# Output tiles counted until stored, z projections and the residual gate across periods, new durations in an own scheduler

## The chip, the cores and the metric

The kernel runs on one core of one Trainium2 chip. The metric is the device time of one execution in microseconds, lower is better. Three runs of the kernel before took 1211.33, 1213.61 and 1215.69 us; the median is 1213.61.

## The reference

One layer (DEPTH is 1, so the gated DeltaNet alone) on x of 1024 x 1024, all float32:

```python
mod = silu(c) @ ada_w + ada_b;  shift, scale, gate = split(mod, 3)
h = rms_norm(x, norm_g) * (1 + scale) + shift
qkv, z, b_lin, a_lin = split(h @ w_in)            # 8 q/k heads, 16 v heads of 128
qkv = silu(causal_conv(qkv, conv_w))              # 4 taps
q, k = l2norm(q) * 128**-0.5, l2norm(k)           # each used by 2 value heads
beta = sigmoid(b_lin);  g = -exp(a_log) * softplus(a_lin + dt_bias)
gc = cumsum(g) in a chunk; decay = exp(gc_i - gc_j)
t_mat = inverse(I + strictly_lower(beta k k^T * decay))
for chunk:                                        # state S, 128 x 128 for a head
    v_new = u - w @ S;  o = q_dec @ S + qk @ v_new
    S = S * exp(g_last) + k_dec^T @ v_new
out = rms_norm(x + gate * ((rms_norm(o, norm_w) * silu(z)) @ w_out), final_g)
```

## The kernel before

The heads are worked in eight **pairs** (two value heads that share one q/k head), numbered 0 to 7. Chunks of 128 tokens give each pair eight scan steps. Products in float32 precision of the big matrices are three passes of 128x512 matmuls on split values (`whi`, `wlo` and the high and low halves of h): a tile of 128 columns and 512 tokens is 24 matmuls (L598, "projection matmuls").

**Stages of a pair.** Its k and q tiles (4 projections) and v tiles (4) pass a convolution on VectorE (three steps L557 a tile, after L552 and L554 on ScalarE, before the SiLU L561), and are transposed (k and q L659, L667; v L813, then `vtok` L816). `stage_a` takes products of k and q (L704) and makes eight `at` tiles in two halves (L706, L710). They go to DRAM (D<-at, L715) and come back in another layout (`ua`, L724). On `ua` VectorE inverts 32 x 32 blocks in 62 dependent steps (L733 and L736 in turn, of growing and shrinking size). The result goes through DRAM (D<-tb L738, TT<-D L755), is transposed (L758 to L760), and `levels` joins the blocks to 128 x 128 on TensorE (L766, L768, L778, L779, L789, L797 with copies between), for one half of the tokens and then for the other. Then the pair's `scan` may start: a step is L963, L982, L940, L973, L910 on TensorE with small VectorE and ScalarE work between.

**The scan's output.** After a step the output `o` is normed; `finish` transposes it into the PSUM bank `pot` (L892), ScalarE writes `oT` (L896), GpSimd multiplies it by `z` (L897), and SyncE stores it to `o_dram` (L898). `pot` has one buffer, `oT` two, and up to ZB = 3 tiles of z are fetched ahead. `out_gate` makes z for a head: two projections, SiLU (L868), a store to `z_dram` (L865).

**The residual gate** is gate = silu(c) @ ada_w's third part: for each of eight column tiles two loads of 256 KB (`wag`, L1007), eight products on VectorE (L1011, L1013), a sum (L1016), a reduction on TensorE (L1020) and an add (L1022); at the end a transpose (L1026). `wag` has one buffer (WGB), and a tile's first load waits for the tile before.

**The order.** All five engines take their instructions in the order in which the program emits them. A planner sets it in Python. Work is written as generators that yield None after a matmul or a condition to wait for. `drive` steps the first generator of a list that can go on; a clock `now` advances by a matmul's cost. VectorE, ScalarE, GpSimd and SyncE operations go into queues (`put`) with a cost, a rank and the operations they come after; `advance` emits from each queue, at the planned time, the ready operation of lowest rank. `done` asks if an operation ended LATP ago, `avail` if a tag has a buffer whose readers are done. The costs are AC, VC, LAT, DMA and the numbers beside the calls.

**Periods.** The outer loop has nine periods gi = -1 to 7. In a period the scan of pair gi, `stage_a` of pair gi + 1 and, as filler, projections run: the z heads of the period (ZQ gives 3, 2, 2, 2, 2, 2, 2, 1, 0 of them), the v tiles of pair gi + 1 and the k and q tiles of pair gi + 2. A period ends when all its generators in `must` are over. `residual_gate` is in `must` of period RG = 1. In period 6 `early` (output products L1066 of the first four heads) may take NE = 15 steps behind the fillers; it runs free in period 7. After the periods the rest of the output product follows: 768 matmuls in all, L1066.

## Time and profile before

| | |
|---|---|
| profiled execution, its own time | 1215.66 us |
| its span, first to last instruction | 1213.9 us |
| TensorE matmul busy | 1090.0 us (90%) |
| VectorE / ScalarE / GpSimd busy | 752.1 / 542.3 / 436.0 us |
| mean granted TensorE clock | 0.947 |
| SyncE's queue q1 | 117.15 MB, 33.8% of 16 engines' span |

The time is the slowest core's, here the only one's, and the span is the part of it between the first and the last instruction. The engines overlap, so their busy times do not add up. A matmul's row covers its passage through the array: matmuls start every 0.23 us while each row lasts 0.4, and "busy" is the time that at least one covers. The granted clock is 1.0 at 2.4 GHz and 0.5 at 1.2 GHz; a mean in between is a mix of both.

### The profile page before, as it was taken

How to read it: one execution, taken by the hardware profiler on the slowest of the kernel's cores; microseconds unless marked ns; L12 is line 12 of the kernel's file. 1: busy time of each engine (PE TensorE's matmuls, PEld its weight loads, DVE VectorE, ACT ScalarE, POOL GpSimd, SP SyncE). 2: the span in 40 equal slices, each digit the busy share in tenths (PEclk: the TensorE clock that was granted, in tenths of full speed). 3: DMA queues.
4: the chain of work that ended last, by engine and by line, in shares of the span. 5: the costliest groups of instructions: out<-in, count | busy, mean ns of one | idle time of the engine just before them, and what ended most of it. 6: DMA issues, size and time to landing. Idle time of an engine off the chain costs nothing.

```text
span 1213.9 us, 18304 instructions
## 1 busy us (share of the span) xinstructions
PE 1090.0 (90%) x6295; PEld 870.9 (72%) x6295; DVE 752.1 (62%) x1913; ACT 542.3 (45%) x1415; POOL 436.0 (36%) x530
## 2 busy tenths in 40 slices
PE   8998986999998949999899989998998849999997
PEld 7877764777776737777677767776776637788775
DVE  5457864685758747766586767586665854512614
ACT  5466821443652326336623733473365312514433
POOL 3442320431452215313521442163126123754653
PEclk8899996999998969999999989998999878999999
DMA  9712141241243421421424042214213260536441
GB/s 291 194 35 96 32 119 31 70 117 45 79 125 90 107 72 55 127 61 58 109 61 118 19 125 61 84 45 125 62 57 107 88 198 17 182 102 183 152 130 70
DMA packets 187555, 118.43 MB, mean 98 GB/s; under 512 B 59669, under 2 KB 166470, under 8 KB 186438
## 3 DMA queue, kind: packets, MB, share of 16 engines
q1 hardware_dynamic: 186960, 117.15, 33.8%
q8 instruction: 50, 0.82, 0.3%
q14 instruction: 43, 0.35, 0.1%
q10 hardware_dynamic: 502, 0.10, 0.0%
HBM read 91.98 MB, written 25.24 MB: 97 GB/s over the span
## 4 chain that ended last, share of the span: by engine, by line
PE 46%; DVE 18%; ACT 15%; DMA 8%; issue 6%; POOL 5%; SPq 2%; DVEq 0%; POOLq 0%; ACTq 0%
PE pj L598 24%; PE pj L1066 3%; DVE tm L733 2%; DVE vT L557 2%; DVE tb L736 2%; DMA woraw<-in_gdn_w_out 2%; DVE kq L557 2%; DVE em L641 2%; PE tr L797 2%; POOL wolo L206 2%; PE tr L789 2%; ACT tr L669 2%; DMA o_dram<-oT 2%; ACT tr L662 1%; ACT junk L918 1%
## 5 line engine op out<-in xcount | busy, mean ns | idle before, releaser
L587 POOL TENSOR_TENSOR wlo<-wraw,whi 128x512 fp32r<-128x512 f32 x88 | 116.2, 1336 | 317.1 <-ACT whi L586 305.0
L733 DVE TENSOR_TENSOR tm<-tb,ua 128x126 f32<-128x126 f32 (+22 forms) x248 | 88.7, 358 | 52.7 <-DMA ua<-D 46.4
L557 DVE SCALAR_TENSOR_TENSOR kq<-xb,taps,kq 128x512 f32<-128x512 f32 x96 | 78.3, 825 | 30.4 <-ACT kq L554 23.5
L557 DVE SCALAR_TENSOR_TENSOR vT<-xb,taps,vT 128x512 f32<-128x512 f32 x96 | 78.3, 816 | 20.0 <-ACT vT L554 19.0
L736 DVE TENSOR_TENSOR tb<-tb,tm 128x126 f32<-128x126 f32 (+22 forms) x248 | 83.8, 338 | 7.1
L552 ACT COPY xb<-pj 128x512 f32<-128x512 f32 x62 | 36.3, 585 | 101.1 <-PE pj L598 97.4
L598 PE MATMUL pj<-h0hib,wlo 128*128 128x512 f32 x184 | 79.0, 429 | 0.0
L598 PE MATMUL pj<-h0hib,whi 128*128 128x512 f32 x184 | 78.4, 426 | 0.0
L598 PE MATMUL pj<-h0hia,whi 128*128 128x512 f32 x184 | 77.0, 418 | 1.3 <-ACT kq L554 1.3
L598 PE MATMUL pj<-h0lob,whi 128*128 128x512 f32 x184 | 77.8, 423 | 0.0
L598 PE MATMUL pj<-h1hib,wlo 128*128 128x512 f32 x184 | 77.3, 420 | 0.0
L598 PE MATMUL pj<-h1loa,whi 128*128 128x512 f32 x184 | 77.1, 419 | 0.0
L598 PE MATMUL pj<-h1hib,whi 128*128 128x512 f32 x184 | 76.4, 415 | 0.0
L598 PE MATMUL pj<-h1hia,wlo 128*128 128x512 f32 x184 | 76.0, 413 | 0.0
L922 POOL TENSOR_TENSOR sso<-sso,neg_half 128x2 f32<-128x2 f32 x64 | 45.0, 705 | 84.9 <-DVE sso L920 76.1
L598 PE MATMUL pj<-h1lob,whi 128*128 128x512 f32 x184 | 75.4, 410 | 0.0
L598 PE MATMUL pj<-h0loa,whi 128*128 128x512 f32 x184 | 75.1, 408 | 0.0
L598 PE MATMUL pj<-h1hia,whi 128*128 128x512 f32 x184 | 74.8, 407 | 0.0
L598 PE MATMUL pj<-h0hia,wlo 128*128 128x512 f32 x184 | 74.6, 406 | 0.0
L951 POOL TENSOR_TENSOR sg<-st,eall 128x256 f32<-128x256 f32 x48 | 30.2, 629 | 103.8 <-ACT st L985 103.8
L206 POOL TENSOR_TENSOR wolo<-woraw,wohi 128x512 fp32r<-128x512 f32 x36 | 48.1, 1356 | 46.8 <-ACT wohi L205 46.8
L897 POOL TENSOR_TENSOR oT<-oT,z 128x256 f32<-128x256 f32 x64 | 47.7, 746 | 45.1 <-ACT oT L896 44.1
(460 smaller groups left out, 2930.9 us busy)
## 6 DMA issues: line engine op xcount, KB each, us to landing
wraw<-in_gdn_w_in SPq DMA_DIRECT2D x92, 256.0 KB, 3.6
woraw<-in_gdn_w_out SPq DMA_DIRECT2D x50, 256.0 KB, 3.0
wa<-in_ada_w SPq DMA_DIRECT2D x16, 512.0 KB, 7.1
em<-gc_dram SPq DMA_DIRECT2D x8, 1024.0 KB, 5.3
z_dram<-sz SPq DMA_DIRECT2D x32, 256.0 KB, 2.4
z<-z_dram SPq DMA_DIRECT2D x64, 128.0 KB, 2.4
o_dram<-oT SPq DMA_DIRECT2D x64, 128.0 KB, 2.2
gsrc<-o_dram SPq DMA_DIRECT2D x32, 256.0 KB, 3.1
```

Source lines behind the costliest of these rows:

```text
L206: nc.gpsimd.tensor_tensor(lo, raw, hi.bitcast(F32), op=ALU.subtract)
L552: a = act(lambda: nc.scalar.copy(xb[:, NTAP - 1:], ps), 512, *old, rank=0, holds=held)
L557: d = [vec(lambda j=j: nc.vector.scalar_tensor_tensor(dst, xb[:, j:j + TH], tp[:, j], dst, op0=ALU.mult, op1=ALU.add), 512, *d)]
L587: ops.append(pool(lambda raw=raw, ks=ks, hi=hi, lo=lo: nc.gpsimd.tensor_tensor(lo[:, ks], raw, hi[:, ks].bitcast(F32), op=ALU.subtract), 1 ...
L598: nc.tensor.matmul(ps, lhsT=a[:, k], rhs=b[half][k // 4][:, k % 4], start=(k == 0 and n == 0), stop=(k == KT - 1 and n == 2))
L641: e = [vec(lambda n=n, h=h: nc.vector.scalar_tensor_tensor(em[:, h, n], em[:, h, n], ngc[:, n, h0 + h:h0 + h + 1], mask, op0=ALU.add, op1= ...
L733: d = [vec(lambda j=j, mm=mm, ln=ln, tmv=tmv: nc.vector.tensor_tensor(tmv, tb[:, :mm, j:j + 1].to_broadcast([P, mm, ln]), ua[:, j:j + 1, j ...
L736: d = [vec(lambda j=j, mm=mm, tmv=tmv: nc.vector.tensor_tensor(tb[:, :mm, j + 1:], tb[:, :mm, j + 1:], tmv, op=ALU.subtract), 170 + mm * l ...
L897: b = pool(lambda: nc.gpsimd.tensor_tensor(oT, oT, z, op=ALU.mult), 800, a, zo)
L922: d = pool(lambda: nc.gpsimd.tensor_tensor(sso, sso, neg_half[:, :2], op=ALU.pow), 700, d)
L951: sgo = pool(lambda n=n, sg=sg: nc.gpsimd.tensor_tensor(sg, st, gle[:, n, hs, None].to_broadcast([P, 2, P]), op=ALU.mult), 800, rank=0)
L1066: nc.tensor.matmul(acc, lhsT=a[:, ts], rhs=b, start=(first and n == 0), stop=(last and n == 2))
```

## The change

- `oT` gets three buffers (OB), and a buffer counts as taken until its store is over (`order.hold("oT", 1)`, asked in `can_finish`); in the kernel before the planner did not ask. z tiles fetched ahead: ZB 5 for 3.
- The z heads of each period become a run of their own (`zruns`). Their own period still needs them (`follow` steps the run to its end), and the period before may work on them when nothing else can go on.
- `residual_gate` runs in the background, in no period's `must`. `wag` has two buffers (WGB = 2), and a load waits for the operations of the load two before; a first product waits for the tile before.
- `early` runs without a quota from period 6 on (`take` and the NE steps are gone).
- Planned durations: LAT is 200 (150) between engines and 50 on one engine, LATP 320 (250), some costs of ScalarE and VectorE, and the 62 inversion steps 220 + n/2 (170 + 3n/4).
- The builder's `dynamic_dma_scratch_size` is set to 1024.

```diff
-LAG, ZB, WGB = 3, 3, 1
+LAG, ZB, WGB, OB = 3, 5, 2, 3
-LAT, LATP, DMA = 150, 250, 2800
+LATS, LAT, LATP, DMA = 50, 200, 320, 2800
-AC = {512: 530, 256: 400, 128: 240}
-VC = {512: 690, 256: 340, 128: 265}
+AC = {512: 560, 256: 400, 128: 250}
+VC = {512: 750, 256: 360, 128: 280}
...
-            t = max(t, a.end + LAT)
+            t = max(t, a.end + (LATS if a.eng == self.eng else LAT))
...
-                op=ALU.mult), 170 + mm * ln * 3 // 4, *d, rank=2)]
+                op=ALU.mult), 220 + mm * ln // 2, *d, rank=2)]
...
-            oT = cp.tile([P, 2, P], F32, name="oT", tag="oT")
+            oT, stored = cp.tile([P, 2, P], F32, name="oT", tag="oT", bufs=OB), order.hold("oT", 1)
...
-                out=o_dram[h0:h0 + 2, :, n * P:(n + 1) * P].rearrange("h e t -> e h t"), in_=oT), b)
+                out=o_dram[h0:h0 + 2, :, n * P:(n + 1) * P].rearrange("h e t -> e h t"), in_=oT), b, holds=stored)
...
-            return late and late[0][0] in zs and done(late[0][2]) and free("pot")
+            return late and late[0][0] in zs and done(late[0][2]) and free("pot") and order.avail("oT", OB)
...
-                d = load(lambda wa=wa, k4=k4, i=i: nc.sync.dma_start(out=wa, in_=av[:, k4:k4 + 4, 2, i]), d)
+                old, mine = ring("wag", WGB)
+                d = load(lambda wa=wa, k4=k4, i=i: nc.sync.dma_start(out=wa, in_=av[:, k4:k4 + 4, 2, i]), *old)
...
+    def follow(run):
+        while not run.over:
+            yield lambda: run.over or not run.wait or run.wait()
+            run.step()
...
+    gate_heads, zruns = iter(zgates), []
+    for n in ZQ:
+        zruns.append(Run(itertools.chain(*itertools.islice(gate_heads, n))))
...
-            zfill = itertools.chain(*zgates[:ZQ[gi + 1]])
-            del zgates[:ZQ[gi + 1]]
+            zfill = follow(zruns[gi + 1])
...
-                    more = itertools.chain(done_projecting(), take(tail, NE))
+                    more = done_projecting()
...
             if gi == RG:
-                streams.append(residual_gate())
+                background.append(Run(residual_gate()))
             must = [Run(g) for g in streams] + [Run(itertools.chain(*filler))]
-            drive(background + must + ([trun] if gi == HQ - 1 else []), must)
+            drive(background + must + ([zruns[gi + 2]] if gi + 2 < len(zruns) else []) + [trun] * (gi >= HQ - 2), must)
```

Lines after the gate's loop move down by one: L1020, L1026 and L1066 are L1021, L1027 and L1067 in the changed kernel.

**TensorE at the end of the residual gate** (between the last join of pair 2's inversion, L797, and the first steps of its scan, L963). Before:

```order
L789 MATMUL tr<-TE,at 64x64 x8
L797 MATMUL tr<-TT_731,pn_4028 64x64 x8
L1020 MATMUL tr<-ones,accg 128x1 x2
L1026 MATMUL tr<-ident,gate_c 8x128
L963 MATMUL ts<-vtok,TT_730 128x128 x2
L659 MATMUL tr<-ident,kq 128x128 x4
```

In the change:

```order
L797 MATMUL tr<-TT_731,pn_4075 64x64 x8
L1021 MATMUL tr<-ones,accg 128x1
L963 MATMUL ts<-vtok,TT_730 128x128 x2
L598 MATMUL pj<-h0lob,whi 128x512
L598 MATMUL pj<-h0hib,wlo 128x512
L598 MATMUL pj<-h1hia,whi 128x512
L1027 MATMUL tr<-ident,gate_c 8x128
L659 MATMUL tr<-ident,kq 128x128 x4
```

Two reductions and the transpose stood ahead of the scan's first product; now one reduction does, and the transpose has three projection matmuls and that product ahead of it.

**ScalarE at the end of a scan** (the last `oT` tiles and the z heads' SiLU, of the scan of pair 4; the scans after are alike). Before:

```order
L975 ACTIVATE o<-oq,eall 128x128 x2
L896 ACTIVATE oT<-pot,cols 128x256
L918 ACTIVATE junk,sso<-o 128x128 x2
L868 ACT_TABLE_LOAD
L868 ACTIVATE sz<-pj 128x512
L896 ACTIVATE oT<-pot,cols 128x256 x2
L586 CAST whi<-wraw 128x512 x2
L896 ACTIVATE oT<-pot,cols 128x256
L868 ACTIVATE sz<-pj 128x512 x2
```

In the change:

```order
L868 ACT_TABLE_LOAD
L868 ACTIVATE sz<-pj 128x512
L896 ACTIVATE oT<-pot,cols 128x256
L918 ACTIVATE junk,sso<-o 128x128 x2
L969 ACTIVATE vh<-ts,brk 128x128 x2
L975 ACTIVATE o<-oq,eall 128x128 x2
L586 CAST whi<-wraw 128x512 x2
L896 ACTIVATE oT<-pot,cols 128x256
L918 ACTIVATE junk,sso<-o 128x128 x2
L896 ACTIVATE oT<-pot,cols 128x256
L868 ACTIVATE sz<-pj 128x512
L896 ACTIVATE oT<-pot,cols 128x256
```

Two oT in a row are now apart: the next but one has a z head's SiLU, and with it a projection, ahead of it.

**VectorE in the inversion** (the first v tile's convolution L557 among the 62 steps L733 and L736 of pair 5; its neighbours are alike). Before:

```order
L736 TENSOR_TENSOR tb<-tb,tm 128x9x14
L733 TENSOR_TENSOR tm<-tb,ua 128x130
L736 TENSOR_TENSOR tb<-tb,tm 128x10x13
L557 SCALAR_TENSOR_TENSOR vT<-xb,taps,vT 128x512
L733 TENSOR_TENSOR tm<-tb,ua 128x120
L557 SCALAR_TENSOR_TENSOR vT<-xb,taps,vT 128x512
```

In the change:

```order
L736 TENSOR_TENSOR tb<-tb,tm 128x11x10
L733 TENSOR_TENSOR tm<-tb,ua 128x108
L557 SCALAR_TENSOR_TENSOR vT<-xb,taps,vT 128x512
L736 TENSOR_TENSOR tb<-tb,tm 128x12x9
L557 SCALAR_TENSOR_TENSOR vT<-xb,taps,vT 128x512
L733 TENSOR_TENSOR tm<-tb,ua 128x96
```

The convolution stood behind 38 steps of the inversion and now stands behind 45.

## Rows read from the trace of the kernel before

**Rows 1.** Windows of one stage each: start:end, length, busy, clock, DMA.

```profile
core 0: us, PE busy (x) PEld busy (x) DVE busy (x) ACT busy (x) POOL busy (x), PEclk, DMA share, GB/s
152.80:191.20 38.40, 23.49 (x101) 18.59 (x99) 21.63 (x67) 6.20 (x11) 7.69 (x6) 0.85 0.38 102
191.20:221.30 30.10, 27.09 (x272) 22.69 (x273) 17.74 (x51) 8.16 (x28) 5.12 (x8) 0.80 0.11 24
221.30:269.70 48.40, 45.39 (x216) 36.72 (x214) 35.13 (x99) 20.42 (x61) 20.67 (x30) 0.96 0.38 101
269.70:351.50 81.80, 76.07 (x523) 60.44 (x523) 54.22 (x138) 41.41 (x123) 27.77 (x36) 1.00 0.25 71
351.50:412.30 60.80, 56.02 (x246) 44.22 (x246) 45.34 (x135) 21.87 (x45) 16.53 (x21) 0.94 0.43 117
412.30:484.90 72.60, 53.56 (x414) 43.33 (x414) 44.49 (x138) 32.59 (x108) 22.08 (x28) 0.86 0.25 71
484.90:534.90 50.00, 46.52 (x215) 36.78 (x213) 37.12 (x94) 18.81 (x40) 16.71 (x23) 1.00 0.39 98
534.90:592.90 58.00, 57.23 (x443) 45.92 (x442) 39.89 (x113) 34.48 (x112) 22.09 (x31) 1.00 0.21 65
592.90:647.00 54.10, 48.63 (x216) 38.13 (x214) 37.18 (x93) 19.75 (x43) 16.84 (x23) 0.97 0.37 93
647.00:704.10 57.10, 56.19 (x436) 45.14 (x436) 40.24 (x111) 33.60 (x110) 21.22 (x29) 1.00 0.21 64
...
816.10:871.70 55.60, 49.63 (x216) 38.93 (x216) 36.35 (x92) 19.83 (x43) 16.14 (x22) 0.94 0.36 90
...
928.80:998.30 69.50, 46.81 (x185) 34.68 (x184) 43.94 (x103) 23.08 (x47) 19.15 (x23) 0.86 0.50 153
998.30:1213.90 215.60, 201.09 (x1037) 162.28 (x1037) 84.48 (x146) 78.13 (x187) 109.84 (x101) 0.96 0.38 119
```

**Rows 2.** TensorE's waits: for what, us in total, times, longest.

```profile
PE tr L766 <- DVE TE L758: 24.5, 2, 15.0
PE pot L892 <- ACT oT L896: 20.0, 6, 4.9
PE tr L1020 <- DVE accg L1016: 17.8, 4, 7.6
...
PE tr L813 <- ACT vT L561: 4.6, 5, 1.0
```

**Rows 3.** The chain of waits, 81 projection matmuls on end: start, us.

```profile
294.28 18.91 PE pj L598 x81
```

**Rows 4.** Timeline of TensorE behind a hole: start, us, instruction.

```profile
112.37 0.63 PE L598 MATMUL pj<-h0hib,wlo 128*128 128x512 f32 x1
112.80 0.63 PE L598 MATMUL pj<-h0hib,whi 128*128 128x512 f32 x1
```

**Rows 5.** Timeline of VectorE, the inversion of pair 4.

```profile
593.78 0.60 DVE L706 SCALAR_TENSOR_TENSOR at<-tr,brk,em 128x128 f32<-128x128 f32 x2
...
605.01 0.19 DVE L733 TENSOR_TENSOR tm<-tb,ua 128x31 f32<-128x31 f32 x1 [6.98 <-DMA ua<-D]
...
638.05 0.19 DVE L736 TENSOR_TENSOR tb<-tb,tm 128x16 f32<-128x16 f32 x1
...
641.44 2.33 DVE L557 SCALAR_TENSOR_TENSOR vT<-xb,taps,vT 128x512 f32<-128x512 f32 x3 [1.44 <-ACT vT L554]
644.65 0.43 DVE L758 STREAM_TRANSPOSE TE<-TT 32x256 f32<-32x256 f32 x1 [0.88 <-DMA TT<-D]
```

**Rows 6.** Timeline of VectorE, the inversion of pair 0.

```profile
185.10 0.18 DVE L736 TENSOR_TENSOR tb<-tb,tm 128x16 f32<-128x16 f32 x1
190.68 0.43 DVE L758 STREAM_TRANSPOSE TE<-TT 32x256 f32<-32x256 f32 x1 [5.40 <-DMA TT<-D]
```

**Rows 7.** Timeline of VectorE, the gate's last products.

```profile
447.54 1.14 DVE L1013 SCALAR_TENSOR_TENSOR accg<-wag,cols,accg 128x128 f32<-128x128 f32 x4 [2.98 <-DMA wag<-in_ada_w]
```

**Rows 8.** Timeline of ScalarE at the end of a scan.

```profile
716.31 0.47 ACT L896 ACTIVATE oT<-pot,cols 128x256 f32<-128x256 f32 x1 [5.07 <-DMA o_dram<-oT]
```

More of the change, by code (lines that the diff above doesn't have):

```diff
@@ L734, in stage_a @@
                 tmv, tb[:, :mm, j:j + 1].to_broadcast([P, mm, ln]), ua[:, j:j + 1, j + 1:].to_broadcast([P, mm, ln]),
-                op=ALU.mult), 170 + mm * ln * 3 // 4, *d, rank=2)]
+                op=ALU.mult), 220 + mm * ln // 2, *d, rank=2)]
             d = [vec(lambda j=j, mm=mm, tmv=tmv: nc.vector.tensor_tensor(
-                tb[:, :mm, j + 1:], tb[:, :mm, j + 1:], tmv, op=ALU.subtract), 170 + mm * ln * 3 // 4, *d, rank=2)]
+                tb[:, :mm, j + 1:], tb[:, :mm, j + 1:], tmv, op=ALU.subtract), 220 + mm * ln // 2, *d, rank=2)]
         G.d2 = [load(lambda p=p: nc.sync.dma_start(out=D2[:, :, :, p, :].rearrange("u b m i -> (u b) m i"),
@@ L1003, in residual_gate @@
             accs = cp.tile([P, 2, P], F32, name="accg", tag="accg", bufs=1)
-            d = last
             for k4 in range(0, KT, 4):
                 wa = cp.tile([P, 4, P], F32, name="wag", tag="wag", bufs=WGB)
-                d = load(lambda wa=wa, k4=k4, i=i: nc.sync.dma_start(out=wa, in_=av[:, k4:k4 + 4, 2, i]), d)
+                old, mine = ring("wag", WGB)
+                d = load(lambda wa=wa, k4=k4, i=i: nc.sync.dma_start(out=wa, in_=av[:, k4:k4 + 4, 2, i]), *old)
                 for k in range(k4, k4 + 4):
@@ L1014, in residual_gate @@
                             a, wa[:, k - k4], cols[:, k:k + 1], a, op0=ALU.mult, op1=ALU.add)
-                    d = vec(f, 128, d, rank=3)
+                    d = vec(f, 128, d, *([last] if k < 2 else []), rank=3)
+                mine.append(d)
             d = vec(lambda accs=accs: nc.vector.tensor_tensor(accs[:, 0], accs[:, 0], accs[:, 1], op=ALU.add), 128, d,
@@ L1181, in early @@
                     yield None
-    def take(g, n):
-        for y in g:
-            yield y
-            n -= y is None
-            if n == 0:
-                return
     class Run:
@@ L1219, in gdn_layer @@
     background = [Run(loader()), Run(early_loads())]
-    tail = early()
-    trun = Run(tail)
+    trun = Run(early())
+    gate_heads, zruns = iter(zgates), []
+    for n in ZQ:
+        zruns.append(Run(itertools.chain(*itertools.islice(gate_heads, n))))
     rows = []
@@ L1331 @@
     from concourse.bass_utils import run_bass_kernel_spmd
-    nc = bacc.Bacc("TRN2", target_bir_lowering=False, num_devices=1)
+    nc = bacc.Bacc("TRN2", target_bir_lowering=False, num_devices=1, dynamic_dma_scratch_size=1024)
     arrays, args = {}, []
```

## The prediction

> **What bounds the kernel now.** I read the busy table first, then the windows by stage, then TensorE's waits, then the timeline around each long wait. S stands for the last L704 of a pair and T for its first L766; the windows are cut there [rows 1]. In the windows T to S of the later pairs TensorE works 56.2 of 57.1 us, so there TensorE is the bound. Its idle time lies in a few places: in 152.8 to 191.2 (23.5 of 38.4 us busy), in 412.3 to 484.9 (53.6 of 72.6), in the windows S to T of pairs 4 to 6 (5.5 us in pair 4, 6.0 in pair 6), and before the T of pair 7 (46.8 of 69.5). The waits name the places [rows 2]: L766 waits for TE, that is for the end of the inversion (15.0 us for pair 0, the remaining 9.5 for pair 7), the transposes L892 wait for oT (20.0 us in six waits), and L1020 waits for the gate's accg (17.8 us). After such holes the clock is at its lower level: 0.80 in 191.2 to 221.3, 0.86 in 412.3 to 484.9 [rows 1]. A projection matmul starts 0.233 us after the one before at the full clock (18.91 us for 81) [rows 3] and 0.43 us after it at 1.2 GHz [rows 4], so each us at the lower level loses 0.46 us of projections.
>
> **What stands beside the bubble.** The oT wait of pair 4 to 6 lies inside the window S to T, and another chain runs through the same window. For pair 4 the last `at` ends at 594.4, the inversion's first step starts at 605.0 when `ua` has landed, its 62nd ends at 638.2, and L758 starts at 644.65 [rows 5]; T is 647.0 [rows 1], 54.1 us after S. L758 and its two neighbours take 0.43 us each, so TE was ready at about 646.1 and the slack is only some 1 us. That decides what the third oT buffer is worth.
>
> **The change, part by part.** The numbers of instructions are counted in the two programs' orders; durations are from rows.
>
> (1) z projections run ahead. Between S and T of pair 0 stand 148 projection matmuls, 99 before. The 49 added are 49 x 0.233 = 11.4 us of work in a hole of 15.0 us. T itself does not move: the inversion alone sets it (VectorE has nothing else to do in it, and L758 starts at 190.7 [rows 6]), so this window stays 38.4 us with some 3.5 us idle. What is won comes later. The window to S of pair 1 gets 17 more matmuls (+4.0), keeps 4.6 us of the 12 at the lower clock (0.80 over 30.1 us; -3.4), and its small waits of 2 us are filled by projections between the inversion's stages: 30.1 becomes 28.7. From S to T of pair 1 nine convolution steps (0.78 us each, 2.33 for three [rows 5]), three `vtok` products and two copies (some 2.4 together) now stand between the inversion's steps, 9.4 us more in a chain that ended last already (48.4 us): 57.0, a little less than the sum because waits inside it overlap. The window after it has 75 matmuls fewer (-17.5) and one set of transposes fewer (-2.9): 81.8 becomes 61.
>
> (2) Residual gate. It no longer holds back the end of its period, and its loads come in pairs. TensorE idles 19.0 us of 412.3 to 484.9 [rows 1], the most of it for accg, behind single loads (VectorE idles 2.98 us before the last four products [rows 7]). The orders show the next scan's L963 directly behind one reduction. I take away 16 us of idle time and 3.2 us of low clock, add 21 matmuls (4.9) and leave 1 us: 58.5. The window before it (4.8 us idle) loses the rest of that wait, but its VectorE chain holds 28 gate products instead of 20: 60.8 to 59.5.
>
> (3) Third oT buffer. The wait is oT's store (ACT idle 5.07 us until o_dram<-oT is over [rows 8]). The planner now spaces the last transposes by 6 and 18 matmuls instead of 4, 12 and 4, and three buffers cover a store. I take the wait as gone. What is late next is the inversion: S to T of pairs 4 to 6 now holds 151 projection matmuls, 180 before, and with the transposes and scan products in between (some 6 us) about 41.3 us of TensorE work. The chain through the same window, from pair 4's rows: 1.5 us from S to the last `at`; then 9.5 to the first step (10.6 before, where the order has two weight loads just ahead of `ua`'s; now a z store and a z load); 62 steps, 33.2 us before with nine convolution steps (7.0), two `vtok` and a copy (some 1.6) among them, so 24.6 without these, now with six steps (4.7), one `vtok` and a copy (0.8) and one wait for a tile less (0.6): 29.5; then 6.4 for the two DMAs to L758, and 0.5. Sum 47.4. TensorE stands still for 5 to 6 us again, only at another instruction: the first tile's convolution comes behind 45 of the steps (38 before), so its transposes L813 wait. I take 48.0 with the lower clock. The bounds are 42 (the chain runs early, TensorE alone) and 52 (the chain as long as before less its slack). The window T to S gets the 29 matmuls that left: 57.1 + 5.9 + 1.0 for clock = 64. A period is then 112.0, and was 112: the bubble of 4.4 us buys nothing here.
>
> The Trainium skill (Perfetto Trace Analysis, Optimization Strategy) says that the same gap, repeated on the engine that should be busy, can mean too few buffers for the next tile. By it the third buffer would be worth the whole gap; the trace shows the gap, and beside it a chain with 1 us of slack. What that makes of the time is the first rival.
>
> (4) Tail. `early` may start in the period of pair 6 without a quota: 66 output matmuls stand before the T of pair 7, 45 before. They wait for the weights' loads as before, but 21 x 0.233 = 4.9 us fill part of the 9.5 us before T: 69.5 becomes 67.5 and the rest has 4.9 less to do, and, by estimate, 3.4 less at the lower clock (half of what 0.96 over 215.6 us makes, as the hole before it is half as long) and 2 less of gaps between the inversion's stages, which six matmuls each now fill: 215.6 becomes 205.3.
>
> (5) The scheduler's durations alone change nothing that computes; their effect is the orders counted above. The smaller DMA scratch I cost at nothing, between -1 and +1: no wait of the trace names it.
>
> **Sum.** Windows before and forecast (the start up to S of pair 0 first): 152.8/152.0, 38.4/38.4, 30.1/28.7, 48.4/57.0, 81.8/61.0, 60.8/59.5, 72.6/58.5, 50.0/49.5 (seven matmuls fewer, but the inversion sets it), 58.0/54.1 (17 matmuls moved away), S to T of pairs 4 to 6 (54.1, 54.9, 55.6) 164.6/144.0, T to S, three of 57.1, 171.3/192.0, 69.5/67.5, 215.6/205.3. Together 1213.9 becomes 1167.5, 46.4 less. The profiled execution took 1215.66, 2.05 over the median of the three runs, so on the runs' scale I forecast 1213.6 - 46.4 = 1167 us.
>
> **Rivals.**
> *TensorE alone is the bound.* If the inversion is early enough everywhere, nothing replaces the holes: 6.5 less from S to T of pair 1, 3 each for pairs 2 and 3, 18 and 4.5 in the three later periods: 35 less, 1132. For it: nothing else in the windows T to S waits. Against it: the slack of 1 us in rows 5. Chance 0.2. The page named above would have it so.
> *The gate's holes stay.* DVE takes the gate's products last of all, and the loads stand in one queue behind them; if each pair is late by its landing, some 14 of the 17.8 us return: 1181. For it: L1020 waited four times, up to 7.6 us. Against: two buffers halve the trips. Chance 0.1.
> *The convolution becomes the loop.* L813 waits where a tile's steps, the SiLU and the transposes run one behind the other instead of beside the next tile. It now waits at most 1.0 us, five times [rows 2]. If all four tiles of a pair pay the 2.3 us of three steps and as much for the activations around them, that is 4.2 x 4 = 17 us in each of seven pairs, where I have counted 5: 84 more, 1251. It is slower than before from 46.4/7 = 6.6 us above my count in each pair. For it: DVE takes the tile's steps behind more inversion steps. Against: only the first tile meets a full chain. Chance 0.05.
> *The change does nothing*, because the inversion sets every period: then T of pair 0 and the gate would have to be hidden as well, which their 15.0 and 17.8 us speak against. Chance 0.03.
>
> **How the numbers follow.** Forecast 0.62, with its own range of 1150 to 1184; the rivals 0.2, 0.1, 0.05, 0.03. The range for 8 in 10 runs from 1136, the edge of the first rival with part of its gains, to 1190, past the gate's return. 0.3% of this kernel is about what can be told from no change (3.6 us). Faster: 0.62 + 0.2 + 0.1 = 0.92; same 0.03; slower 0.05.
>
> **What would show it.** T of pair 0 still near 191, with L766 waiting under 5 us; L1020 (now L1021) waiting under 4 us in total; hardly any wait of L892 for oT; and in the later periods waits of 3 to 6 us at L813 and L766, with the period between 110 and 113 us. Periods near 105 us would prove the first rival; L1021 still above 10 us the second; waits at three or four L813 in each period the third.

## The result, and the profile after

The changed kernel took 1155.97 us (median of 4 runs, 1154.56 to 1157.00), the kernel before 1212.47 us beside it (4 runs, 1208.99 to 1215.69). The ratio is 0.9534, 95% interval 0.9504 to 0.9563. The forecast was 1167 us with a range of 1136 to 1190. The profiled execution took 1154.56 us, its span 1152.8 us against 1213.9. Of the kernels below, g_warm has one slow execution of 2626.28 us, which its ratio leaves out.

The windows by stage of the changed kernel, cut at S and T as in [rows 1] (columns as there; the first one starts with the kernel):

```profile
0.00:146.70 146.70, 134.81 (x703) 109.83 (x703) 97.53 (x228) 96.62 (x199) 53.95 (x73) 0.95 0.47 134
146.70:185.10 38.40, 34.92 (x152) 27.83 (x150) 21.61 (x67) 6.79 (x12) 7.77 (x6) 1.00 0.38 102
185.10:220.30 35.20, 34.50 (x290) 27.55 (x291) 18.25 (x52) 10.44 (x33) 7.61 (x10) 0.76 0.22 58
220.30:275.70 55.40, 49.97 (x247) 39.59 (x247) 45.69 (x116) 24.33 (x68) 24.23 (x34) 1.00 0.37 93
275.70:332.80 57.10, 54.91 (x427) 43.71 (x428) 43.15 (x118) 32.68 (x106) 21.09 (x27) 1.00 0.26 78
...
391.70:457.70 66.00, 60.22 (x429) 48.29 (x429) 42.45 (x123) 33.32 (x106) 23.30 (x30) 0.90 0.29 82
...
563.40:607.90 44.50, 41.12 (x191) 32.49 (x189) 34.91 (x93) 17.21 (x38) 15.46 (x21) 1.00 0.39 101
607.90:672.20 64.30, 61.76 (x461) 49.86 (x461) 43.54 (x111) 36.49 (x115) 23.86 (x30) 1.00 0.23 66
...
890.50:951.20 60.70, 52.12 (x207) 38.51 (x206) 44.47 (x110) 22.82 (x47) 20.95 (x25) 0.86 0.58 176
951.20:1152.80 201.60, 190.09 (x1017) 153.85 (x1016) 81.16 (x144) 78.14 (x187) 108.59 (x100) 0.99 0.40 126
```

Against [rows 1] the largest gains are T to S of pair 1 to 2 (81.8 to 57.1), the end (215.6 to 201.6), S to T of pairs 4 to 6 (54.1 to 44.5 in pair 4) with the window behind it longer (57.1 to 64.3), and S to T of pair 7 (69.5 to 60.7). Two windows grew: behind T of pair 0 (30.1 to 35.2) and S to T of pair 1 (48.4 to 55.4). Next, TensorE's waits, the rows that answer to [rows 2] (for what, us in total, times, longest):

```profile
PE tr L813 <- ACT vT L561: 16.1, 11, 2.9
PE oq L973 <- DVE o L913: 7.7, 6, 1.6
...
PE tr L766 <- DVE TE L758: 3.5, 1, 3.5
...
PE tr L1021 <- DVE accg L1017: 1.8, 2, 1.4
...
PE pot L892 <- POOL o L923: 1.5, 1, 1.5
```

L766 fell from 24.5 to 3.5 us, the gate's wait from 17.8 to 1.8, and the 20.0 us for oT are gone; L813 rose from 4.6 to 16.1. TensorE's idle gaps sum to 68.7 us (115.6 before), and 69.5 us run at the lower clock (129.8 before).

### The profile page after: what moved, and what is told of

Same layout as the page of the kernel before. It is cut to its first block, busy times and chain, and to the rows that moved or that the text cites. A ratio compares the mean times of both kernels' runs of the same rounds, so it can differ in the third digit from the quotient of the medians.

```text
span 1152.8 us, 18300 instructions
## 1 busy us (share of the span) xinstructions
PE 1075.8 (93%) x6295; PEld 859.8 (75%) x6295; DVE 757.8 (66%) x1913; ACT 542.7 (47%) x1415; POOL 440.1 (38%) x530
## 4 chain that ended last, share of the span: by engine, by line
PE 43%; DVE 23%; ACT 11%; DMA 8%; issue 6%; POOL 6%; SPq 2%; DVEq 0%; ACTq 0%; POOLq 0%
PE pj L598 20%; DVE tm L733 5%; DVE tb L736 5%; PE pj L1067 4%; DVE vT L557 3%; DMA ua<-D 2%; DVE em L641 2%; DMA woraw<-in_gdn_w_out 2%; POOL wolo L206 2%; PE tr L704 2%; PE tr L797 2%; PE tr L789 2%; ACT tr L662 1%; ACT tr L669 1%; DVE kq L557 1%
## 5 line engine op out<-in xcount | busy, mean ns | idle before, releaser
L587 POOL TENSOR_TENSOR wlo<-wraw,whi 128x512 fp32r<-128x512 f32 x88 | 120.1, 1380 | 301.0 <-ACT whi L586 291.3
L733 DVE TENSOR_TENSOR tm<-tb,ua 128x126 f32<-128x126 f32 (+22 forms) x248 | 81.2, 327 | 25.3 <-DMA ua<-D 18.9
L557 DVE SCALAR_TENSOR_TENSOR kq<-xb,taps,kq 128x512 f32<-128x512 f32 x96 | 76.4, 804 | 22.3 <-ACT kq L554 19.2
L736 DVE TENSOR_TENSOR tb<-tb,tm 128x126 f32<-128x126 f32 (+22 forms) x248 | 82.2, 331 | 6.9
L557 DVE SCALAR_TENSOR_TENSOR vT<-xb,taps,vT 128x512 f32<-128x512 f32 x96 | 82.1, 855 | 5.0 <-ACT vT L554 3.9
L598 PE MATMUL pj<-h0loa,whi 128*128 128x512 f32 x184 | 78.6, 427 | 0.0
L598 PE MATMUL pj<-h0hia,wlo 128*128 128x512 f32 x184 | 77.2, 419 | 0.0
L598 PE MATMUL pj<-h0hib,wlo 128*128 128x512 f32 x184 | 76.0, 413 | 0.0
L598 PE MATMUL pj<-h0hib,whi 128*128 128x512 f32 x184 | 74.7, 406 | 0.0
L598 PE MATMUL pj<-h1hib,wlo 128*128 128x512 f32 x184 | 74.6, 405 | 0.0
L897 POOL TENSOR_TENSOR oT<-oT,z 128x256 f32<-128x256 f32 x64 | 48.1, 751 | 51.7 <-ACT oT L896 44.9
L896 ACT ACTIVATE oT<-pot,cols 128x256 f32<-128x256 f32 x64 | 30.3, 474 | 78.5 <-PE pot L892 76.8
```

Source lines behind the costliest of these rows:

```text
L557: d = [vec(lambda j=j: nc.vector.scalar_tensor_tensor(dst, xb[:, j:j + TH], tp[:, j], dst, op0=ALU.mult, op1=ALU.add), 512, *d)]
L587: ops.append(pool(lambda raw=raw, ks=ks, hi=hi, lo=lo: nc.gpsimd.tensor_tensor(lo[:, ks], raw, hi[:, ks].bitcast(F32), op=ALU.subtract), 1 ...
L598: nc.tensor.matmul(ps, lhsT=a[:, k], rhs=b[half][k // 4][:, k % 4], start=(k == 0 and n == 0), stop=(k == KT - 1 and n == 2))
L733: d = [vec(lambda j=j, mm=mm, ln=ln, tmv=tmv: nc.vector.tensor_tensor(tmv, tb[:, :mm, j:j + 1].to_broadcast([P, mm, ln]), ua[:, j:j + 1, j ...
L736: d = [vec(lambda j=j, mm=mm, tmv=tmv: nc.vector.tensor_tensor(tb[:, :mm, j + 1:], tb[:, :mm, j + 1:], tmv, op=ALU.subtract), 220 + mm * l ...
L896: a = act(lambda: nc.scalar.mul(oT, pot, normw_c), 470, holds=held)
```

## The experiments

Six kernels undo one part or do one alone, and g_after is the control of two of them (u_gate and u_dur); five more take up what these left open. No run takes out the smaller DMA scratch by itself. Numbers of matmuls in a window, idle time and time at the lower clock are counted in the traces. One thing is needed to read the totals: u_oT below has the same instructions in the same order as the changed kernel, and its runs take 1146.6 to 1160.1 us. Differences under 1% are therefore read from windows first. A window has one profile for each kernel, and one window of one order can differ by its clock (under g_after, 60.6 to 68.4 us), so a window counts most where several kernels agree.

**a_oT: the buffers (of oT and z) and the DMA scratch, on the kernel before.**

```diff
-LAG, ZB, WGB = 3, 3, 1
+LAG, ZB, WGB, OB = 3, 5, 1, 3
```

with the hold on `oT`. ZB and `dynamic_dma_scratch_size=1024` go along, which the expectation doesn't say.

> The kernel before with three oT buffers in place of two (and the planner's count of them, which moves nothing: the instructions stand in the order of before on all five engines). Theory A (my prediction: beside the wait for oT's store runs the inversion's chain with 1 us of slack): ACT's wait for o_dram<-oT (21.6 us, 6 times) and TensorE's wait at L892 (20.0 us, 6 times) go, but TensorE then waits at L766 or L813 of the same pair for nearly as long; -1 to -6 us against before, ratio 0.995 to 0.999. Rival B (the bubble is the bound, one buffer is all that lacks): -15 to -20 us, ratio 0.984 to 0.988. Rival C (the store's wait was the DMA queue and not the buffer, so the wait stays): ratio 0.999 to 1.001, ACT's wait unchanged.

Measured: 1191.74 us, ratio 0.9834 (0.9795 to 0.9873): 21.0 us by medians (1212.75 beside it), Rival B's size; my theory A is out. Windows of a_oT, S to T of pair 4 and T to S behind it, then TensorE's L813 wait and ScalarE's for the store:

```profile
587.80:637.40 49.60, 47.20 (x216) 37.10 (x215) 34.83 (x93) 20.06 (x43) 17.06 (x23) 1.00 0.39 100
637.40:694.50 57.10, 56.24 (x438) 45.25 (x437) 40.32 (x112) 33.54 (x111) 21.28 (x29) 1.00 0.22 65
```

```profile
PE tr L813 <- ACT vT L561: 10.2, 10, 1.5
```

```profile
ACT oT L896 <- DMA o_dram<-oT: 6.1, 3, 2.3
```

S to T fell by 4.5 us with nothing given back behind it, and in pairs 5 and 6 by 5.4 and 6.1. The inversion, which I had put beside the wait with 1 us of slack, became shorter by itself. Its steps and the convolution between them in pair 4, VectorE, first before (605.0 to 638.2) and then in a_oT (599.3 to 628.6); columns: instructions, busy us, mean ns, idle before them:

```profile
L733 DVE TENSOR_TENSOR tm<-tb,ua 128x126 f32<-128x126 f32 (+22 forms) x31 | 11.4, 369 | 7.8 <-DMA ua<-D 7.0
L736 DVE TENSOR_TENSOR tb<-tb,tm 128x126 f32<-128x126 f32 (+22 forms) x31 | 10.3, 332 | 1.0
L557 DVE SCALAR_TENSOR_TENSOR vT<-xb,taps,vT 128x512 f32<-128x512 f32 x9 | 7.8, 862 | 1.5 <-ACT vT L554 1.5
```

```profile
L733 DVE TENSOR_TENSOR tm<-tb,ua 128x126 f32<-128x126 f32 (+22 forms) x31 | 10.4, 337 | 7.1 <-DMA ua<-D 6.3
L736 DVE TENSOR_TENSOR tb<-tb,tm 128x126 f32<-128x126 f32 (+22 forms) x31 | 8.9, 286 | 1.0
L557 DVE SCALAR_TENSOR_TENSOR vT<-xb,taps,vT 128x512 f32<-128x512 f32 x9 | 7.8, 861 | 0.3 <-ACT vT L554 0.2
```

The same 62 steps take 2.4 us less, the convolution waits 1.2 us less for ScalarE: the chain contained the wait. From first step to last it takes 29.3 us for 33.2, in pairs 5 and 6 29.2 for 34.2 and 29.1 for 34.3. While ScalarE stands at L896, the activations and weight casts behind it are late, TensorE's next tile is late, so VectorE waits for L554; and the late GpSimd work falls beside the steps (k_pool below). In the kernel before four steps stand beside that late work (L897, L587, L897 from 605.78 to 609.71) and take 3.69 us; in a_oT the same four take 1.37. Two rows of the kernel before:

```profile
606.51 2.51 POOL L587 TENSOR_TENSOR wlo<-wraw,whi 128x512 fp32r<-128x512 f32 x2
606.66 1.20 DVE L736 TENSOR_TENSOR tb<-tb,tm 128x58 f32<-128x58 f32 x1
```

What this run does not part is oT's buffers from z's. In the kernel before SyncE waited for a free z buffer:

```profile
SPq L885 <- POOL oT L897: 34.5, 14, 5.6
```

a_oT has no such row. A z that comes late makes the multiplication late, and then the store; which of the two buffers is worth how much of the 20 us stays open. The smaller scratch is in this run too. Windows that hold little or no oT wait stand as before (T to S of pair 1 to 2 81.6 us for 81.8, the end 215.4 for 215.6), so no gain of the scratch is seen there; it was not tried alone.

**u_oT: two oT buffers in the changed kernel.** `OB = 2`, and `can_finish` doesn't ask for a free one.

> The changed kernel with two oT buffers in place of three and without the planner's count of them; the instructions stand in the same order on all five engines, so the buffer alone is tried. Theory A (my prediction's step: the wait for oT's store is real, but the inversion's chain runs beside it): ACT waits for o_dram<-oT at L896 again and L892 with it, some 3 to 5 us in each of pairs 4 to 6, where the L813 wait of 2.8 us then shrinks; time +0 to +6 us, 1156 to 1162. Rival B (nothing runs beside it): the 20 us of before come back in full, 1172 to 1178. Rival C (the new order alone spaces the transposes enough): no wait for oT, within 1 us of 1156.

Measured: 1152.74 us (1146.56 to 1160.14), ratio 0.9496 (0.9458 to 0.9534), no slower than the changed kernel. ScalarE waits for the store nearly as long as in the kernel before (21.6 us, 6 times):

```profile
ACT oT L896 <- DMA o_dram<-oT: 18.6, 7, 3.9
```

yet no row has TensorE waiting for oT. So Rival C holds for TensorE, and its time is missed by less than the runs of this kernel spread; ScalarE's wait, which C also took away, stays. The new order puts 6 and 18 projection matmuls between the last transposes, and ScalarE's wait ends before TensorE needs `pot`. The order and the buffers remove the same bubble; beside the order (and z's five tiles, which this run keeps) the third oT buffer has no measurable worth.

**u_z: no z projections of the next period.** `[zruns[gi + 2]]` is taken out of what `drive` may run.

> The changed kernel without the z projections of the next period in what may run in this one. 44 projection matmuls move from in front of pair 0's T to behind it, and like moves follow in later periods. Theory A (my prediction: T0 is set by the inversion alone and the z products fill the hole): L766 of pair 0 waits 3.5 + 44 x 0.228 = 13.5 us again, T0 stays within 1 us of 185.0, the lower clock after it stays, and the time is 8 to 14 us more, 1164 to 1170. Rival B (the run-ahead only moves work between windows, the inversion bounds the periods anyway): within 3 us of 1156. Rival C (the products lie in the chain's way: run-ahead costs time from S to T of pair 1, 48.4 before and 55.4 now): faster than 1156 by up to 5 us.

Measured: 1172.36 us, ratio 0.9660 (0.9628 to 0.9692), 16.4 us over the changed kernel. Windows S to T of pair 0 and T to S behind it, and TensorE's wait:

```profile
148.50:187.00 38.50, 24.66 (x106) 19.53 (x105) 21.65 (x67) 6.29 (x11) 7.72 (x6) 0.87 0.38 102
187.00:218.00 31.00, 28.36 (x275) 23.88 (x276) 18.47 (x52) 8.11 (x29) 5.12 (x8) 0.77 0.11 24
```

```profile
PE tr L766 <- DVE TE L758: 16.4, 3, 13.9
```

The window stays 38.5 us with 10.3 us less in it, as theory A has it (13.9 us of wait for 13.5). The time is 2 us over A's range; the lower clock lasts 91.4 us in all, 69.5 in the changed kernel.

**g_after: a control.** `second` returns the addition L913, and the scan goes on to L973 when `read.end is not None`.

> The changed kernel with one condition more in the scan: L913, which reads the last oq tile, has been placed before L973 writes the next. The control for u_dur and u_gate. Theory A: the planner held most of this order anyway, TensorE's wait for o at L973 (7.7 us, 6 times) falls by up to 5 us, and the time is 0 to 5 us below 1156. Rival B: the products that go in front of L973 only move the waits, within 2 us of 1156.

Measured: 1146.19 us, ratio 0.9456 (0.9425 to 0.9487). The wait fell from 7.7 to 1.7 us and the time by more than A said:

```profile
389.60:445.60 56.00, 54.32 (x426) 43.33 (x426) 42.44 (x124) 33.06 (x103) 21.94 (x28) 1.00 0.33 95
```

```profile
PE oq L973 <- DVE o L913: 1.7, 5, 0.5
```

The window is T to S of pair 2 to 3: 56.0 us at clock 1.00 where the changed kernel takes 66.0 at 0.90, with 4 us less idle time in it. Not all of the 10 us is the condition's. u_oT, which has the changed kernel's order, took 60.6 us for this window, none of it at the lower clock:

```profile
387.60:448.20 60.60, 54.64 (x429) 43.61 (x429) 42.69 (x124) 33.23 (x106) 23.37 (x30) 1.00 0.31 90
```

With the order of the changed kernel it takes 60.6 to 68.4 us (the changed kernel, u_oT, u_tail, k_warm, k_pool), with the condition 55.8 to 56.4 (g_after, g_warm, n_late), so 4 us are the condition's in any case, and the rest is the clock, which one run of that order pays and another doesn't.

**u_gate: the old residual gate** (`streams.append(residual_gate())`, WGB 1, one load behind the other, on g_after).

> The changed kernel with the old residual gate: one wag buffer, each load behind the last product of the one before, and the gate among the streams that must end in their period; with g_after's condition in the scan. Theory A (my prediction: the gate's loads and its place at the period's end made 16 us of idle time and 3 us of lower clock): L1020 waits 10 us or more again and the time is 12 to 20 us over g_after. Rival B (the z products that may now run across the period fill the gate's holes, so the period's end costs nothing): L1020 waits but the time is within 4 us of g_after. Rival C (the gate only moves its 64 products on DVE into another pair's inversion): slower windows S to T of pairs 2 and 3 in one of the two kernels, within 4 us.

Measured: 1182.34 us, ratio 0.9747 (0.9712 to 0.9783), 36 us over g_after: more than any theory. Windows T to S of pairs 2 to 3 and 6 to 7, and waits:

```profile
385.90:464.30 78.40, 75.61 (x519) 60.78 (x519) 50.00 (x144) 38.19 (x111) 22.72 (x27) 1.00 0.31 91
855.40:916.70 61.30, 50.43 (x389) 43.45 (x389) 35.27 (x105) 30.76 (x101) 18.42 (x27) 0.78 0.20 58
```

```profile
PE tr L766 <- DVE TE L758: 16.2, 5, 7.3
...
PE tr L1020 <- DVE accg L1016: 5.8, 5, 1.7
```

The gate itself makes only 5.8 us of wait. But its period lasts until it is done, and in that time the z projections of later periods run: 204 projection matmuls in the first window, 107 in g_after. The 97 more, 22.6 us at 0.233, are all of the 22.4 by which it is longer, and they are missing later: 62 matmuls for 139 in the second window, where L766 waits and the clock is 0.78. Rival B had the z products fill the holes; they fill one and open others. Three things are undone at once here (the second buffer, the loads' order, the place in `must`), and they are not parted. Nor is 36 us what the gate's part is worth on the kernel before: there a period had only its own z heads as filler, so its gate could not spend those of later periods.

**u_dur: the old durations** (both tables, latencies, inversion steps; on g_after).

> The changed kernel with the old durations throughout (the two tables, one latency of 150 for every step, 250 for TensorE's waits, the old cost of the inversion's steps); one condition is added to the scan, that the addition L913 which reads the last oq tile has been placed before L973 writes the next (g_after has that condition alone and is the one to compare with). Theory A (the new order comes mostly from the durations: they keep oT's transposes apart and the scan's products from being placed before their inputs): TensorE waits for oT or vT, 20 us or more, come back; 10 to 25 us slower than g_after. Rival B (my prediction, which gave the durations nothing of their own): within 4 us of g_after. The start should show it too: L400 waited 3.56 us before and 1.09 after.

Measured: 1167.98 us, ratio 0.9630 (0.9598 to 0.9661), 21.8 us over g_after: A's size, but not by the waits that A named (L813 waits 17.8 us, 15.4 in g_after; L892 waits 2.8 us for oT, not at all there). The start and S to T of pair 2, and the wait at L400 in the start:

```profile
0.00:153.10 153.10, 140.57 (x708) 114.20 (x708) 97.05 (x228) 96.77 (x199) 53.79 (x73) 0.93 0.45 129
...
338.10:404.20 66.10, 59.00 (x275) 46.09 (x274) 54.61 (x161) 25.45 (x59) 21.70 (x29) 1.00 0.39 101
```

```profile
PE ts L400 <- DVE gg L396: 3.6, 1, 3.6
```

The start is that of the kernel before again (152.8), so a part of the 6 us gained there is the durations'. How much is less sure than two profiles make it look: the three profiles with the old durations have 149.9 (a_oT) to 153.1 us, the ten with the new ones and the old load of ua in pair 0 have 145.3 to 148.8, 4.9 us apart in the mean. In pairs 1 to 6 S to T is longer (66.1 for 57.4 in pair 2) and T to S behind it shorter; up to S of pair 4 this costs 11.7 us net, and from there to S of pair 7 nothing (331.1 us with either).

**u_tail: output products one period later** (`[trun] * (gi >= HQ - 1)`).

> The changed kernel with the early output products started one period later, in the last period as before, but without the old quota of 15. Theory A (the 9.5 us hole in front of pair 7's T is filled by these products): L766 of pair 7 waits 5 to 9 us again, S7 to T7 grows from 60.7 us, the part behind it gets the products and a little lower clock; time +5 to +10 us, 1161 to 1166. Rival B (the hole is gone because the z products of the last periods moved, and the output products wait for their weights wherever they stand): within 2 us of 1156.

Measured: 1178.21 us, ratio 0.9713 (0.9691 to 0.9736), 22 us over the changed kernel. S to T of pair 7, and the rest:

```profile
884.00:943.50 59.50, 29.30 (x140) 22.95 (x139) 39.48 (x105) 22.80 (x47) 15.92 (x21) 0.78 0.59 180
943.50:1170.10 226.60, 211.69 (x1082) 170.75 (x1082) 86.34 (x149) 78.71 (x187) 113.14 (x104) 0.95 0.36 112
```

```profile
PE tr L766 <- DVE TE L758: 28.0, 2, 24.0
```

TensorE waits 24.0 us for the inversion, and 66 matmuls (15.4 us) move behind it, with more time at the lower clock. This undoes more than the change did: the kernel before had 45 of the 66 there by its quota, so 21 of them (4.9 us) are the change's own.

**k_warm: the hole of pair 0 filled with idle products.**

```diff
+        for _ in range(14 if (gi, hf) == (0, 0) else 0): nc.tensor.matmul(pa0[:, 0], lhsT=ones, rhs=ident, start=True, stop=True)
```

> The changed kernel, with 14 matmuls of 128x128 (ones by ident, into the tr tile that L766 writes next) put in front of pair 0's first L766; nothing else moves. In the changed kernel TensorE waits 3.48 us there and then runs at the lower clock for 17.1 us (185.6 to 202.7). Theory A (the idle time lets the clock fall): 14 x 0.22 = 3.0 us of it is filled, T stays at 185.0, the lower clock after it is gone, T0 to S1 falls from 35.3 us to about 27, and the time by 7 to 9 us, from 1156.0 to about 1148. Rival B (the 32x32 products of L766 to L779, not the wait, let the clock fall): the lower clock stays, time within 1 us of 1156. Rival C (the level falls because of idle time before the wait, in the gates and transposes before 181): the same as B.

Measured: 1150.33 us, ratio 0.9473 (0.9445 to 0.9500). First the changed kernel (the wait, and the first half of the 35.2 us behind T; the second half has clock 1.00), then k_warm (S to T of pair 0, and T to S behind it):

```profile
181.60:185.10 3.50, 0.04 (x2) 0.07 (x2) 0.43 (x1) 0.00 (x0) 0.00 (x0) 1.00 0.38 60
185.10:202.70 17.60, 16.90 (x122) 13.04 (x123) 4.29 (x10) 2.70 (x5) 2.50 (x2) 0.52 0.29 78
```

```profile
148.50:187.30 38.80, 38.11 (x179) 31.11 (x179) 21.78 (x68) 6.79 (x12) 7.78 (x6) 1.00 0.38 102
187.30:215.10 27.80, 27.17 (x289) 22.06 (x290) 18.22 (x52) 10.54 (x32) 7.68 (x10) 1.00 0.27 73
```

The same 34 projection matmuls and small products take 27.8 us at clock 1.00 in place of 35.2 at 0.76. Theory A holds in the window: the 32x32 products alone don't bring the clock down, and with the idle time in front of T filled it stayed up. g_warm and n_late, which have the 14 products too, bear it out (28.0 and 28.2 us, none at the lower clock), while every profile with a wait of 2.3 us or more in front of T (ten of them) has 9 us or more at the lower clock behind it. The idle time need not lie in front of T: u_dur has none there, but 1.50 us at L778 behind it, and then 10.2 us at the lower clock. The total is 5.6 us better, but u_oT without any idle products came out at 0.9496, so it is not settled by the total.

**g_warm: both.** g_after with k_warm's line.

> g_after (the changed kernel with the condition on L913 in the scan) with the 14 matmuls of k_warm in front of pair 0's first L766. Theory A (both gains are independent: the scan's order from pair 2 on, the clock behind T0): L766's wait of 3.5 us and the lower clock of 17.1 us behind it go, T0 to S1 falls from 35.2 us to about 28, and the time from 1146 to about 1139. Rival B (what is won at the clock there comes back as a fall elsewhere): the lower clock in all stays near 70 us and the time within 2 us of 1146.

Measured: 1145.88 us, ratio 0.9445 (0.9416 to 0.9474), no different from g_after. T to S behind pair 0 is 28.0 us as in A, and the lower clock in all 56.4 us against 70.7, but the profiled span is only 2.8 us shorter. Inconclusive on the total.

**n_ua46: a longer planned load of ua** (`order.put("sp", UA, ...)` with UA = 4600 for L724, on g_after).

> g_after with the planner told 4600 in place of 2800 for the loads of ua, so that its inversion starts as late behind the last at as the trace shows it (7.8 us; its own sum was 6.1). Theory A (TensorE's wait for vT, 15.4 us at 8 L813, comes because the planner has the inversion's steps, and the convolution steps in between, some 2 us too early): L813 waits under 6 us in total, L766 of pair 0 under 2, time 6 to 12 us below g_after, 1134 to 1140. Rival B (the chain itself sets S to T, and a better plan only moves the wait to L766): L813's waits fall and L766's rise by as much, within 3 us of 1146.

Measured: 1165.63 us, ratio 0.9599 (0.9548 to 0.9649), slower than g_after. S of pair 4 to S of pair 7:

```profile
567.30:892.70 325.40, 312.00 (x1967) 250.78 (x1966) 237.41 (x625) 165.18 (x466) 122.14 (x158) 0.99 0.29 79
```

Both theories fall (L813 waits 14.3 us, L766 10.0 for 4.3 in g_after). The three later periods gain 5.7 us (331.1 in g_after), but S to T of pairs 1 and 2 is 5.0 and 9.8 us longer, and 24 fewer matmuls stand in front of pair 7's T.

**n_late: the same for pairs 4 to 6 alone** (`UA if 3 < gi < 7 else DMA`, on g_warm).

> g_warm with the planner told 4600 in place of 2800 for ua's loads in pairs 4 to 6 alone. In n_ua46, where all pairs had it, the periods of pairs 4 to 6 took 106.9 us (109.8 and more in g_after), and the pairs before and the end lost more than that. Theory A (the gain of the later periods stands by itself): S4 to S7 takes 321 us in place of 331 and the time is 6 to 10 us below g_warm, 1136 to 1140. Rival B (filler that the later periods no longer leave over is missing in front of pair 7's T, where n_ua46 waited 7.4 us and lost clock): the gain comes back behind S7, within 3 us of 1146.

Measured: 1139.90 us, ratio 0.9393 (0.9371 to 0.9414): faster than both kernels of this case. S of pair 4 to S of pair 7, in g_warm and in n_late:

```profile
545.40:877.10 331.70, 315.26 (x1952) 251.14 (x1952) 235.26 (x610) 161.50 (x457) 117.51 (x153) 0.98 0.30 80
```

```profile
548.30:872.90 324.60, 310.95 (x1951) 246.50 (x1950) 230.30 (x610) 161.64 (x456) 117.23 (x153) 1.00 0.30 81
```

7.1 us gained in these periods, 6.0 in the median: A, with the end unchanged (204.6 us in both). TensorE's wait at the first L813 of each pair falls from 2.9 to 3.1 us to 1.5 to 1.6, and the 13.6 us at the lower clock that g_warm has in these periods to none, which at 0.46 is 6.3 of the 7.1 us. So most of the gain is clock. That it came of the shorter waits is likely and not shown: the changed kernel waits 2.8 to 2.9 us at each of these L813 and has only 3.4 us at the lower clock there.

**k_pool: GpSimd work beside an inversion.** Six `nc.gpsimd.tensor_tensor(dum, us, us, op=ALU.mult)` behind pair 0's loads of `ua`.

> The changed kernel with six GpSimd multiplications of 128x512 (ua by itself into a scratch tile that nothing reads), which start when pair 0's ua has landed, beside the first steps of its inversion; everything else stands in the same order. In the changed kernel four of these 62 steps take 1.23 to 1.29 us in place of some 0.25, and they are those beside GpSimd's L587. Theory A (a step of the inversion beside a GpSimd tensor_tensor lasts as long as that one): six steps more at 1 us or more, the 62 steps take 27 to 29 us in place of 21.9, T0 moves by 5 to 7 us and L766 waits 9 to 10 us; time +5 to +9 us, 1161 to 1165. Rival B (the long steps have another cause, and GpSimd's work is free): 62 steps in 22 us, time within 2 us of 1156.

Measured: 1157.71 us, ratio 0.9534 (0.9511 to 0.9557). VectorE's steps and GpSimd's work (start, us, instruction):

```profile
157.23 0.91 DVE L736 TENSOR_TENSOR tb<-tb,tm 128x30 f32<-128x30 f32 x1
158.17 0.22 DVE L733 TENSOR_TENSOR tm<-tb,ua 128x58 f32<-128x58 f32 x1
...
159.40 1.08 DVE L733 TENSOR_TENSOR tm<-tb,ua 128x56 f32<-128x56 f32 x1
...
166.51 0.26 DVE L733 TENSOR_TENSOR tm<-tb,ua 128x100 f32<-128x100 f32 x1
```

```profile
155.84 6.82 POOL L729 TENSOR_TENSOR dum<-ua 128x512 bf16<-128x512 f32 x6 [1.86 <-DMA ua<-D]
162.61 3.77 POOL L587 TENSOR_TENSOR wlo<-wraw,whi 128x512 fp32r<-128x512 f32 x3
```

Theory A holds for the chain: 62 steps in 27.6 us for 21.9, S to T 44.0 for 38.4. For the time it is not shown: the profiled span is 4.6 us longer, the medians differ by 1.7 us and the intervals lie over each other.

## Why the prediction was right, and where not

The direction, the range and most places were right; the sum of 1167 is 11 us high. That it came so near is in part luck: some windows were forecast 31.1 us too high in sum, others 16.4 us too low, and only the difference shows in the time.

*(1) z projections.* T of pair 0 did not move (38.4 forecast and measured), L766 waits 3.48 us (some 3.5), S to T of pair 1 took 55.4 (57.0), and u_z shows that these matmuls fill the hole. Mis-sized: the window behind T, "30.1 becomes 28.7". I let 4.6 of 12 us at the lower clock stay, as the hole got smaller; a hole of 3.5 us was followed by 17.1 us, and k_warm shows that without it the window is 27.8. T to S of pair 1 to 2 was better than forecast (57.1 for 61).

*(2) Gate.* "leave 1 us" of L1021 is 1.8. T to S of pair 2 to 3 was forecast at 58.5 and took 66.0: 13.7 us at the lower clock, behind gaps of 1.44 us at L778 and 1.18 at L789, and other waits of the scan. u_oT, with the same order, takes 60.6 without any lower clock, so some 5 of the 7.5 us are clock, and g_after, with fewer waits of the scan, takes 56.0. The step also left out what (1) makes of the gate: once z projections may run ahead, u_gate shows, a gate in `must` spends the filler of later periods.

*(3) oT.* The step "the bubble of 4.4 us buys nothing here" failed. I took the inversion's chain for a neighbour of the wait, by the 1 us of slack in [rows 5]; a_oT shows its steps 3.9 us shorter in pair 4 (33.2 to 29.3) when TensorE's wait is gone (ScalarE still waits 2.2 us for the store), so the wait was part of it. In the changed kernel it is not the third buffer that does it: u_oT, with two, has S to T of pair 4 at 44.6 us too, and has the new order and z's five tiles. My chain of 47.4 us for S to T was 44.6 in the changed kernel: 7.9 us to the first step (9.5 forecast), 27.3 for the steps (29.5), 5.6 to L758 (6.4), but 1.8 from there to T (0.5, though by the same rows TE takes 1.4). The periods took 109 us, not 112. The Trainium skill (Perfetto Trace Analysis, Optimization Strategy) reads a repeated gap as a possible lack of buffers. I had weighed this rule against the slack and let the slack win; a_oT agrees with the rule, 0.9834; u_oT shows that an order which keeps the transposes apart closes the same gap.

*(4) Tail.* S to T of pair 7 took 60.7 (67.5 forecast), since the 5 us I left in front of T are gone; the rest 201.6 (205.3), with 4.6 us at the lower clock for 17.6 before, 6.0 us won where I counted 3.4.

*(5) Durations.* I gave them nothing of their own, but counted their orders in the windows behind the start. The start itself I left at 152.0: it took 146.7. L400 waits 1.1 us for 3.6, and 3.4 us at the lower clock behind it are gone; u_dur has both back. a_oT waits 3.5 us at L400 and has no lower clock behind it, so that part is not sure to be the durations'. I had not compared the orders there. The DMA scratch, which I put at nothing, was not tried alone.

*Sum.* The windows were forecast at 1167.5 and are 1152.8. High: 5.3 at the start, 5.5 from S of pair 1 to S of pair 2, 9.8 in S to T of pairs 4 to 6, 10.5 from S of pair 7 on. Low: 6.5 behind T of pair 0, 7.5 behind T of pair 2, 2.4 in the rest. The first rival (TensorE alone, 1132) came part of the way: pairs 4 to 6 still stop 2.8 us at their first L813. The loop of the convolution (its 4.2 us a tile should by its own terms be 4.6) and the gate's return did not come.

## What to carry to other kernels

Before a chain is called independent of a wait, look whether its own steps became longer or later through the engine that waits: a chain with 1 us of slack shrank by 3.9 us when the wait went. Filler is a stock: a generator that must end in its period may spend what a later hole needs, so an undone part can cost more than its own wait, and parts undone one by one do not add up (here they come to more than the whole change). A small hole is priced with the clock behind it, read from the window after it, and from more than one run: T to S of pair 2 to 3 took 60.6 us in one profile and 68.4 in another, with the same order.

## What the runs showed of the hardware

A VectorE step with two inputs beside a GpSimd tensor_tensor lasted about as long as that one: 0.85 to 1.11 us for 0.2 beside six of 1.04 to 1.12 us (k_pool), one step beside each. The Trainium skill (SBUF — State Buffer, Who interferes with whom) says that such a VectorE instruction contends with a GpSimd one that reads SBUF; the runs agree, and I had not weighed it in the prediction.

Around a hole in front of T of pair 0 TensorE ran at 1.2 GHz (granted 0.5) for 17.1 us in the changed kernel (hole of 3.48 us) and for 10.2 us in u_oT (4.05 us), with the same order. The clock did not fall in k_warm, where 14 idle products stood in the hole. The profiles of the changed kernel and of u_oT differ by 8.0 us in span (1152.8 and 1144.8). Their idle gaps are alike (68.7 and 69.4 us in sum), and the lower clock lasts 69.5 us in one and 50.2 in the other; at 0.46 us lost for each that is 8.9 us. So between these two profiles of one order the clock accounts for the whole difference. What decides whether a hole is followed by 10 us at the lower clock or by 17 is not shown.
